# Splits of x queued behind the last gated block, a norm's offset subtracted in step with its sums, and the new tokens' matmuls placed in a row with cache visits

## The chip, the cores and the metric

The kernel runs on one core of one Trainium2 chip. The metric is the device time of one execution in microseconds (us). Before the change three runs took 1761.49, 1762.09 and 1762.12 us, median 1762.09. The profiled execution took 1763.11 us; its trace spans 1761.3 us from the first to the last instruction.

## What is computed

One layer of a decoder for 256 prompt tokens and 8 samples of 4 new tokens (288 tokens), in float32:

```
z = x @ w_in;  h, Bg, Cg, q, k, v, g_a, g_b = split(z)
ya = Bg * causal_conv3(Cg * h)
yb = dilated sliding-window attention(q, k, v, caches)        # 3 groups of 4 heads, dim 128
x1 = LN1(ALPHA*x + (sigmoid(g_a) * (ya @ w_a) + sigmoid(g_b) * (yb @ w_b)) @ w_out)
a, b = split(x1 @ w_up)
y  = LN2(ALPHA*x1 + (silu(causal_conv3(a)) * b) @ w_down)
```

The outputs are y for both groups, the last rows that enter each convolution, and the key and value windows: of the prompt, and of the samples with the new rows appended. Each sample attends to its cached keys (128 positions a group are used) and to the four new ones.

## The kernel before

**Tiling.** Activations lie by feature: 16 tiles of 128 features by 288 tokens (`KD` = 16, `T` = 288). A *product* is one output tile of 128 features for all 288 tokens. Each float32 operand is held as two parts, a rounded one (`hi`) and the rest (`lo`), and three matmuls make up one k step: hi·hi (L208), hi·lo of x (L209), lo·hi (L210). A product over 16 k steps is 48 matmuls of 128 x 128 by 288 columns. The names `acc` in the profile are the PSUM tiles of products.

**Weights.** `prepare` loads one weight block (1 MB, tile `wst`, three buffers) on SyncE's queue, and `half_block` splits each half: ScalarE casts it to `whi` (L138), VectorE subtracts for `wlo` (L139), four buffers of halves each. `product` prepares the next block when it takes one, so that a block is split while the one before it is multiplied. `split` (L213) does the same for activations, both instructions on L214.

**Order.** The program is written as if in one sequence, and a scheduler that estimates times decides the order of the instructions on each engine. `behind(i, after)` forces instruction i behind another on the same engine without a wait. `in_a_row` does this for a list of TensorE matmuls.

**Sample attention** (`sample_steps`, L406 to 496) is a generator; `product` advances it from time to time, so that its pieces stand between products. A *visit* is a row of matmuls that use two tiles of the key or value cache (tile `cache`, two buffers, 1 MB each, loaded and stored again on SyncE's queue by `fetch_two`). Their stationary operand has 32 columns, so four heads use the four column strips of the array (shape 128*32). Scores of the cached keys come from L421 into a `long` tile (one buffer); the scores of the new keys, `pn`, from L438, also in `long`; then the maximum, the exponential and the sum (L443 to 448), transposes (L451, L453, L461), and the sums over the values: L474 for the cache, L485 for the new tokens.

**FFN.** The hidden width of 44 tiles is worked in three parts (`THIRDS` = 16, 16, 12). In each part `gated` blocks are made first (two up products each, convolution, SiLU, gate; then `split` into `gh`, `gl`, which carry the names `yah`, `yal` in the profile), and then 16 down products add to the residual `dd`. In part 0 the input is LN1's argument not yet normalised (`x_gb`, with two more columns), and LN1 is applied behind the product (`normed`, L732); GpSimd and ScalarE normalise `dd` on the side (L773 to 775, one tile to a gated block). At the first down products the 16 tiles of `dd` are split into `x` for parts 1 and 2 (L781).

**LN2** is accumulated beside part 2's down products. `first` (L622) takes an offset c from tile 0. For tiles 1 to 15, GpSimd subtracts c from the residual (L785) before VectorE adds the product (L786); then `add` (L631) squares the tile on ScalarE (L635, tile `cy`, two buffers) and adds to the two sums on GpSimd (L639, L640). Behind the last product TensorE sums over the features (L648, L649), and `finish_out` normalises and stores y.

Of the kernel before, what the change touches and what calls it, by code (L numbers as in the profile page):

```python
# [13 lines left out]
ALU = mybir.AluOpType  # L14
# [3 lines left out]
P = 128  # L18
# [3 lines left out]
NB, NT = 8, 4  # L22
NS = NB * NT
# [10 lines left out]
NG, NH = 3, 4  # L34
# [49 lines left out]
def layer_kernel(ctx: ExitStack, tc: tile.TileContext, ins, outs):  # L84
# [14 lines left out]
    def sb(pl, shape, tag, dt=F32, bufs=None):  # L99
        return pl.tile(shape, dt, tag=tag, name=nm(tag), bufs=bufs)  # L100
# [4 lines left out]
    def h2(ap):  # L105
        return ap.rearrange("p (h a) -> p h a", h=2)
# [4 lines left out]
    def att(cols=512):  # L111
        return sb(ps, [P, cols], "att", bufs=2)

    def f32(ap):
        return ap.bitcast(F32)
# [13 lines left out]
    def copy_rest(after):  # L129
        if rest[0] < N_REST:  # L130
            n = rest[0]
            rest[0] += 1
            behind(sp.dma_start(outs["o_rest"][n], ins["rest"][n]), after)

    def half_block(st, k0, n):
        hi = sb(wp, [P, HK, P], "whi", F32R, bufs=4)
        lo = sb(wp, [P, HK, P], "wlo", F32R, bufs=4)
        act.copy(hi[:, :n, :], st[:, k0 : k0 + n, :])  # L138
        dve.tensor_tensor(lo[:, :n, :], st[:, k0 : k0 + n, :], f32(hi[:, :n, :]), ALU.subtract)  # L139
        return hi, lo, n  # L140

    def weight_list():
# [70 lines left out]
    def split(hi, lo, src):  # L213
        return act.copy(hi, src), dve.tensor_tensor(lo, src, f32(hi), ALU.subtract)  # L214
# [191 lines left out]
    def sample_steps():  # L406
        fetch_two()
        yield
        row = []
        s = sw2[:, :SW]  # L410
        sbias = cst[:, C_SB : C_SB + SW]
        for g in range(NG):
            qm = by_batch(q_s[:, g])
            cols = P if g == 0 else NT * P
            p = sb(ps, [P, cols], "long", bufs=1)
            for b in range(NB):
                if g > 0 or b % 4 == 0:
                    c = cache_tiles.pop(0)
                o = (b % 4) * NH * P if g == 0 else 0
                for j in range(NH):  # L420
                    row.append(pe.matmul(  # L421
                        p[j * NS : (j + 1) * NS], qm[:, j, b, :], c[:, o + j * cols : o + (j + 1) * cols],
                        start=b == 0, stop=b == NB - 1,
                    ))
                if b == NB - 1 or (g > 0 and b % 2 == 1):
                    in_a_row(row)
                    row = []
                    fetch_two()
                    yield
            sg = s[:, g * P : (g + 1) * P]  # L430
            if g == 0:
                dve.tensor_tensor(sg, p, sbias[:, :P], ALU.add)
            else:
                pick_t(sg, p, sbias[:, g * P : (g + 1) * P])
        pn = sb(ps, [P, NG * NS], "long", bufs=1)
        for j in range(NH):
            for g in range(NG):
                pe.matmul(  # L438
                    pn[j * NS : (j + 1) * NS, g * NS : (g + 1) * NS], q_s[:, g, j, :], k_s[:, g, j, :],
                    start=True, stop=True,  # L440
                )
        dve.tensor_tensor(s[:, NG * P :], pn, sbias[:, NG * P :], ALU.add)
        st = sb(wk, [P, 4], "st", bufs=4)  # L443
        dve.reduce_max(st[:, 0:1], s, AX.X)
        dve.tensor_scalar_mul(st[:, 1:2], st[:, 0:1], -SCALE)
        act.activation(s, s, AF.Exp, bias=st[:, 1:2], scale=SCALE, accum_out=st[:, 2:3])
        dve.reciprocal(st[:, 3:4], st[:, 2:3])
        dve.tensor_scalar_mul(s, s, st[:, 3:4])
        pt = att()
        for g in range(NG):  # L450
            pe.transpose(pt[:, g * P : (g + 1) * P], s[:, g * P : (g + 1) * P], ident)  # L451
        pt2 = att()
        pe.transpose(pt2[: NG * NS, :P], s[:, NG * P :], ident)  # L453
        sT = sw2[:, : NG * P].rearrange("p (g r) -> p g r", g=NG)
        act.copy(sT, pt[:, : NG * P].rearrange("p (g r) -> p g r", g=NG))
        sTn = sw2[: NG * NS, NG * P : NG * P + P]
        act.copy(sTn, pt2[: NG * NS, :P])
        vn = sw2[: NG * NS, NG * P + P : NG * P + P + NH * P].rearrange("p (j d) -> p j d", j=NH)
        pv = att()
        for j in range(NH):  # L460
            pe.transpose(pv[: NG * NS, j * P : (j + 1) * P], v_s[:, j].rearrange("p g r -> p (g r)"), ident)  # L461
        act.copy(vn, pv[: NG * NS].rearrange("p (j d) -> p j d", j=NH))
        o_sb = sw2[:, NG * P + P + NH * P : NG * P + 2 * P + NH * P]
        for g in range(NG):
            sm = by_batch(sT[:, g].rearrange("p (j r) -> p j r", j=NH))
            cols = P if g == 0 else NT * P
            if g < 2:
                p = sb(ps, [P, cols], "long", bufs=1)
            for b in range(NB):
                if g > 0 or b % 4 == 0:  # L470
                    c = cache_tiles.pop(0)
                o = (b % 4) * NH * P if g == 0 else 0
                for j in range(NH):
                    row.append(pe.matmul(  # L474
                        p[j * NS : (j + 1) * NS], sm[:, j, b, :], c[:, o + j * cols : o + (j + 1) * cols],
                        start=b == 0 and g < 2, stop=b == NB - 1 and g == 2,
                    ))
                if b == NB - 1 or (g > 0 and b % 2 == 1):
                    in_a_row(row)
                    row = []  # L480
                    fetch_two()
                    yield
            if g == 0:
                for j in range(NH):
                    pe.matmul(  # L485
                        p[j * NS : (j + 1) * NS], sTn[:, j * NS : (j + 1) * NS], vn[:, j, :], start=False, stop=True
                    )
                act.copy(o_sb, p)
            elif g == 2:
                pick_t(o_sb, p, o_sb)  # L490
        po = att(P)
        pe.transpose(po, o_sb, ident)
        oT = sw[:, :P]
        act.copy(oT, po)
        split(ybh[:, :, SEQ:], ybl[:, :, SEQ:], oT.rearrange("p (j r) -> p j r", j=NH))
        yield
# [117 lines left out]
    class Norm:  # L614
# [16 lines left out]
        def add(self, i):  # L631
            d = dd[:, i]
            last = i == KD - 1
            q = self.s2 if i == 0 else sb(wk, [P, T], "cy", bufs=2)
            act.activation(q, d, AF.Square)  # L635
            if i == 0:
                pool.tensor_copy(self.s1, d)
            elif not last or not self.tail:
                pool.tensor_tensor(self.s1, self.s1, d, ALU.add)  # L639
                pool.tensor_tensor(self.s2, self.s2, q, ALU.add)  # L640
            if i == KD - 2:

                act.activation(lw[:, 3, 0:1], q[:, 0:1], AF.Abs_reciprocal_sqrt)
            if last:
                self.p1, self.p2 = att(T), att(T)
                if self.tail:
                    for p, s, e in ((self.p1, self.s1, d), (self.p2, self.s2, q)):
                        pe.matmul(p, f32(ones_d), s, start=True, stop=False)  # L648
                        pe.matmul(p, f32(ones_d), e, start=False, stop=True)  # L649
                else:  # L650
                    w = sb(wk, [P, 4, T], "cache", F32R, bufs=2)
                    split(w[:, 0:2], w[:, 2:4], lw[:, 0:2])
                    for k in range(4):
                        pe.matmul((self.p1, self.p2)[k % 2], ones_d, w[:, k], start=k < 2, stop=k >= 2)

        def at(self, c, i):
            return prm[:, c + i : c + i + 1]
# [84 lines left out]
    cf = sb(big, [P, KF, 2 + 2 * NB], "qk_s")  # L742
    f = 0
    n2 = Norm(R_LN + 2 * KD, R_LN + 3 * KD, True)
    for part, nf in enumerate(THIRDS):
        gh = sb(big, [P, KD, T], "yah", F32R)
        gl = sb(big, [P, KD, T], "yal", F32R)
        for k in range(nf):
# [16 lines left out]
                gated(gf, y, *normed(pb))  # L765
            else:
                gated(gf, y, pb)
            split(gh[:, k], gl[:, k], gf)
            f += 1
            if part == 0:  # L770

# [6 lines left out]
        for i in range(KD):  # L778
            o = product((h3(gh), h3(gl)))
            if part == 0:  # L780
                split(x[0][:, i], x[1][:, i], h2(dd[:, i]))  # L781
                dve.scalar_tensor_tensor(h2(dd[:, i]), h2(dd[:, i]), ALPHA, o, ALU.mult, ALU.add)
            else:
                if f == KF and i > 0:
                    pool.tensor_tensor(dd[:, i], dd[:, i], n2.c, ALU.subtract)  # L785
                dve.tensor_tensor(h2(dd[:, i]), h2(dd[:, i]), o, ALU.add)  # L786
            if f == KF:
                if i == 0:
                    n2.first()
                n2.add(i)  # L790
    yf = sb(big, [P, KD, T], "yah")
    y_out = outs["o_y"].rearrange("p (k t) -> p k t", k=KD)
    n2.finish_out(yf, y_out)
# [183 lines left out]
```

## Time and profile before

| | before |
|---|---|
| median of 3 runs | 1762.09 us (1761.49 to 1762.12) |
| profiled execution | 1763.11 us, span 1761.3 us, 33600 instructions |
| granted TensorE clock, mean | 0.997 |
| HBM traffic over the span | 389.89 MB read, 94.53 MB written |

The page gives for each engine its busy time and share. PE is TensorE, DVE VectorE, ACT ScalarE, POOL GpSimd, SP SyncE. A row of a timeline gives the start in us from the span's start, the duration, the engine and the line of the kernel, the operation, and the tiles as output<-inputs; in square brackets stands the idle time before it and what ended that. Rows that repeat are merged (xN), and the duration then runs to the end of the last. Matmuls overlap, so their starts are what to compare. A matmul in plain float32 stands twice in the trace: the 12 small matmuls of L438 as 24.

### The profile page before, as it was taken

Reading aid. Unit: us, or ns where it says so; the run is one execution under the profiler, and the core shown is the slowest. Engines: PE = TensorE matmul, PEld = TensorE weight load, DVE = VectorE, ACT = ScalarE, POOL = GpSimd, SP = SyncE. Lnnn points to the kernel's source line nnn. Section 1 sums busy time; section 2 is a strip of 40 time slices with the busy share of each in tenths; the row PEclk is TensorE's granted clock in tenths of the full one; section 3 lists DMA queues with packets and bytes.
Section 4 is the critical chain, followed back from the end, with each engine's and each line's share of the span. In section 5 each row is a group of like instructions: output and inputs, shape, how many; then the busy total and the mean of one; then the engine's idle time right before and its main releaser. Section 6 shows DMA issues by size and latency. Waiting matters only on the chain.

```text
span 1761.3 us, 33600 instructions
## 1 busy us (share of the span) xinstructions
PE 1743.9 (99%) x14269; PEld 1714.4 (97%) x14269; DVE 1008.2 (57%) x1322; ACT 798.4 (45%) x1174; POOL 254.8 (14%) x403
## 2 busy tenths in 40 slices
PE   9999999999999999999999999999999999999996
PEld 9999999999999999999999999999999999999996
DVE  5444455545555444455588888774555554555554
ACT  5444444333434333344445656553454443345444
POOL 0000000000000000001155233310011110011174
PEclk9999999999999999999999999999999999999998
DMA  8477787787787887466766566656565656666662
GB/s 325 173 288 264 271 299 297 265 324 297 271 333 285 304 312 269 150 241 252 269 259 220 210 241 226 229 219 236 219 236 219 236 217 238 217 238 217 223 212 105
DMA packets 60919, 436.25 MB, mean 248 GB/s; under 512 B 7265, under 2 KB 8929, under 8 KB 16865
## 3 DMA queue, kind: packets, MB, share of 16 engines
q1 hardware_dynamic: 59040, 429.40, 65.9%
q10 hardware_dynamic: 1728, 4.72, 0.7%
q8 instruction: 111, 1.82, 0.4%
q14 instruction: 40, 0.32, 0.0%
HBM read 389.89 MB, written 94.53 MB: 275 GB/s over the span
## 4 chain that ended last, share of the span: by engine, by line
PE 96%; POOL 1%; ACT 1%; DVE 1%; issue 0%; DMA 0%; ACTq 0%; DVEq 0%
PE acc L208 31%; PE acc L210 31%; PE acc L209 31%; PE acc L276 1%; PE long L421 1%; PE long L474 1%; POOL dd L785 1%; PE att L362 0%; PE att L326 0%; ACT whi L138 0%; POOL qk_s L549 0%; ACT xh L214 0%; ACT yah L708 0%; DVE dd L684 0%; DMA yah<-in_x 0%
## 5 line engine op out<-in xcount | busy, mean ns | idle before, releaser
L139 DVE TENSOR_TENSOR wlo<-wst,whi 128x1024 fp32r<-128x1024 f32 (+1 forms) x578 | 706.9, 1224 | 617.3 <-ACT whi L138 613.2
L138 ACT CAST whi<-wst 128x1024 fp32r<-128x1024 f32 (+1 forms) x578 | 590.0, 1022 | 871.2 <-PE acc L209 767.7
L208 PE MATMUL acc<-xh,whi 128*128 128x288 f32 (+1 forms) x3216 | 923.0, 287 | 0.0
L210 PE MATMUL acc<-xh,wlo 128*128 128x288 f32 (+1 forms) x3216 | 920.5, 286 | 0.0
L209 PE MATMUL acc<-xl,whi 128*128 128x288 f32 (+1 forms) x3216 | 920.4, 286 | 0.0
L208 PEld LDWEIGHTS acc<-xh,whi 128*128 128x128 f32 x3216 | 607.8, 189 | 7.9 <-ACT h L569 2.5
L210 PEld LDWEIGHTS acc<-xh,wlo 128*128 128x128 f32 x3216 | 607.8, 189 | 0.8 <-issue 0.8
L209 PEld LDWEIGHTS acc<-xl,whi 128*128 128x128 f32 x3216 | 607.9, 189 | 0.3 <-issue 0.2
L208 PE MATMUL acc<-yah,whi 128*128 128x288 f32 x1216 | 348.0, 286 | 0.3 <-ACT yah L214 0.3
L210 PE MATMUL acc<-yah,wlo 128*128 128x288 f32 x1216 | 347.7, 286 | 0.6 <-DVE wlo L139 0.6
L209 PE MATMUL acc<-yal,whi 128*128 128x288 f32 x1216 | 347.6, 286 | 0.0
L208 PEld LDWEIGHTS acc<-yah,whi 128*128 128x128 f32 x1216 | 229.7, 189 | 3.1 <-ACT h L591 2.5
L210 PEld LDWEIGHTS acc<-yah,wlo 128*128 128x128 f32 x1216 | 229.8, 189 | 0.8 <-DVE wlo L139 0.8
L209 PEld LDWEIGHTS acc<-yal,whi 128*128 128x128 f32 x1216 | 229.8, 189 | 0.0
L549 POOL COPY qk_s<-u 128x2 f32<-128x2 f32 x44 | 41.5, 943 | 565.7 <-ACT u L758 441.1
L535 DVE SCALAR_TENSOR_TENSOR cy<-u,prm,cy 128x304 f32<-128x304 f32 x120 | 71.1, 593 | 3.4 <-ACT cy L533 0.7
L606 POOL TENSOR_TENSOR ya<-ya,dd 128x288 f32<-128x288 f32 x16 | 13.6, 851 | 306.0 <-DVE ya L605 306.0
L560 DVE TENSOR_TENSOR ya<-cy,acc 128x144 f32<-128x144 f32 x132 | 25.6, 250 | 33.6 <-PE acc L210 33.6
L549 POOL COPY cm<-u 128x2 f32<-128x2 f32 x16 | 3.0, 185 | 254.3 <-DVE u L574 254.3
L214 ACT CAST yah<-ya 128x288 fp32r<-128x288 f32 x76 | 32.7, 430 | 13.8 <-POOL ya L606 8.3
L214 DVE TENSOR_TENSOR yal<-ya,yah 128x288 fp32r<-128x288 f32 x76 | 34.9, 460 | 1.3 <-ACT yah L214 1.2
L639 POOL TENSOR_TENSOR cache<-cache,dd 128x288 f32<-128x288 f32 x29 | 28.0, 964 | 49.0 <-DVE dd L724 33.5
(179 smaller groups left out, 852.8 us busy)
## 6 DMA issues: line engine op xcount, KB each, us to landing
wst<-in_w_in SPq DMA_DIRECT2D x113, 1024.0 KB, 6.0
wst<-in_w_up SPq DMA_DIRECT2D x88, 1024.0 KB, 4.8
wst<-in_w_down SPq DMA_DIRECT2D x32, 1024.0 KB, 4.8
cache<-in_ck SPq DMA_DIRECT2D x18, 1024.0 KB, 6.4
out_o_ck<-cache SPq DMA_DIRECT2D x18, 1024.0 KB, 9.1
cache<-in_cv SPq DMA_DIRECT2D x18, 1024.0 KB, 6.3
out_o_cv<-cache SPq DMA_DIRECT2D x18, 1024.0 KB, 9.8
wst<-in_w_a SPq DMA_DIRECT2D x16, 1024.0 KB, 4.8
```

The source lines that it names most:

```text
L138: act.copy(hi[:, :n, :], st[:, k0 : k0 + n, :])
L139: dve.tensor_tensor(lo[:, :n, :], st[:, k0 : k0 + n, :], f32(hi[:, :n, :]), ALU.subtract)
L208: pe.matmul(out, hi[:, c, :], xh_k, start=k == 0, stop=False)
L209: pe.matmul(out, hi[:, c, :], xl_k, start=False, stop=False)
L210: last_mm[0] = pe.matmul(out, lo[:, c, :], xh_k, start=False, stop=k == nk - 1)
L214: return act.copy(hi, src), dve.tensor_tensor(lo, src, f32(hi), ALU.subtract)
L276: i = pe.matmul(o[b], first_w(term == 2, b, k), xk, start=k == 0 and term == 0, stop=k == KD - 1 and term == 2)
L421: row.append(pe.matmul(p[j * NS : (j + 1) * NS], qm[:, j, b, :], c[:, o + j * cols : o + (j + 1) * cols], start=b == 0, stop=b == NB - 1,))
L535: dve.scalar_tensor_tensor(y, u[:, i : i + YW], prm[:, w0 + i : w0 + i + 1], y, ALU.mult, ALU.add)
L549: pool.tensor_copy(dst[:, 0:2], u[:, SEQ : SEQ + 2])
L560: dve.tensor_tensor(a, b, c, ALU.mult)
L639: pool.tensor_tensor(self.s1, self.s1, d, ALU.add)
```

## The change

Four edits; none adds or takes away arithmetic.

- `half_block` uses `split` and keeps its two instructions in `w_split`.
- The splits of x in part 0's down products (L781) go behind the split of the last gated block (`last_split`) and behind that of the latest weight block, on ScalarE and VectorE each.
- The subtraction of c (L785) for tile i > 2 goes behind the sum of tile i - 3; `add` returns its last GpSimd instruction for this.
- The new tokens' matmuls L438 and L485 are appended to the row of the last key visit and of the first value visit. `pn` moves to an `att` tile (two buffers), and its loops are turned round, so that the four heads follow each other.

```
-        act.copy(hi[:, :n, :], st[:, k0 : k0 + n, :])
-        dve.tensor_tensor(lo[:, :n, :], st[:, k0 : k0 + n, :], f32(hi[:, :n, :]), ALU.subtract)
+        w_split[:] = split(hi[:, :n, :], lo[:, :n, :], st[:, k0 : k0 + n, :])
...
+                if g == NG - 1 and b == NB - 1:
+                    pn = att(NG * NS)
+                    row += [
+                        pe.matmul(
+                            pn[j * NS : (j + 1) * NS, k * NS : (k + 1) * NS], q_s[:, k, j, :], k_s[:, k, j, :],
+                            start=True, stop=True,
+                        )
+                        for k in range(NG) for j in range(NH)
+                    ]
...
-        pn = sb(ps, [P, NG * NS], "long", bufs=1)
-        for j in range(NH):
-            for g in range(NG):
-                pe.matmul(
-                    pn[j * NS : (j + 1) * NS, g * NS : (g + 1) * NS], q_s[:, g, j, :], k_s[:, g, j, :],
-                    start=True, stop=True,
-                )
...
+                if g == 0 and b == NB - 1:
+                    row += [
+                        pe.matmul(
+                            p[j * NS : (j + 1) * NS], sTn[:, j * NS : (j + 1) * NS], vn[:, j, :], start=False, stop=True
+                        )
+                        for j in range(NH)
+                    ]
...
             if g == 0:
-                for j in range(NH):
-                    pe.matmul(
-                        p[j * NS : (j + 1) * NS], sTn[:, j * NS : (j + 1) * NS], vn[:, j, :], start=False, stop=True
-                    )
                 act.copy(o_sb, p)
...
-                pool.tensor_copy(self.s1, d)
+                i_sum = pool.tensor_copy(self.s1, d)
...
-                pool.tensor_tensor(self.s2, self.s2, q, ALU.add)
+                i_sum = pool.tensor_tensor(self.s2, self.s2, q, ALU.add)
...
-            split(gh[:, k], gl[:, k], gf)
+            last_split = split(gh[:, k], gl[:, k], gf)
...
-                split(x[0][:, i], x[1][:, i], h2(dd[:, i]))
+                for i_x, *before in zip(split(x[0][:, i], x[1][:, i], h2(dd[:, i])), last_split, w_split):
+                    for b in before:
+                        behind(i_x, b)
...
-                    pool.tensor_tensor(dd[:, i], dd[:, i], n2.c, ALU.subtract)
+                    i_c = pool.tensor_tensor(dd[:, i], dd[:, i], n2.c, ALU.subtract)
+                    if i > 2:
+                        behind(i_c, sums[i - 3])
...
-                n2.add(i)
+                sums.append(n2.add(i))
```

More of the change, by code (lines that the diff above doesn't have):

```diff
@@ L133, in copy_rest @@
             behind(sp.dma_start(outs["o_rest"][n], ins["rest"][n]), after)
+    w_split = []
     def half_block(st, k0, n):
@@ L635, in add @@
             act.activation(q, d, AF.Square)
+            i_sum = None
             if i == 0:
-                pool.tensor_copy(self.s1, d)
+                i_sum = pool.tensor_copy(self.s1, d)
             elif not last or not self.tail:
                 pool.tensor_tensor(self.s1, self.s1, d, ALU.add)
-                pool.tensor_tensor(self.s2, self.s2, q, ALU.add)
+                i_sum = pool.tensor_tensor(self.s2, self.s2, q, ALU.add)
             if i == KD - 2:
@@ L654, in add @@
                         pe.matmul((self.p1, self.p2)[k % 2], ones_d, w[:, k], start=k < 2, stop=k >= 2)
+            return i_sum
         def at(self, c, i):
@@ L744, in layer_kernel @@
     n2 = Norm(R_LN + 2 * KD, R_LN + 3 * KD, True)
+    sums = []
     for part, nf in enumerate(THIRDS):
```

## The prediction

> **What bounds the kernel now.** I read the page's engine shares first, then the chain of waits, then TensorE's timeline wherever one of its matmuls starts later than a step after the one before, then the other engines' timelines at those places.
>
> ```profile
> span 1761.3 us, 33600 instructions
> ...
> PE 1743.9 (99%) x14269; PEld 1714.4 (97%) x14269; DVE 1008.2 (57%) x1322; ACT 798.4 (45%) x1174; POOL 254.8 (14%) x403
> ...
> PE   9999999999999999999999999999999999999996
> ```
>
> TensorE has work for all but 17.4 us of the span, and of that the last of the page's 40 slices (44 us each, busy to six tenths) holds most; the change touches nothing behind the last product. So no other engine's time counts by itself. The change can only win where TensorE stands still or runs badly packed matmuls, and only lose where it makes TensorE wait. Its normal step and the first badly packed place stand in one stretch of TensorE's timeline (columns: start, duration, engine, line, operation, count):
>
> ```profile
> 443.24 0.29 PE L209 MATMUL acc<-xl,whi 128*128 128x288 f32 x1
> ...
> 443.73 0.29 PE L210 MATMUL acc<-xh,wlo 128*128 128x288 f32 x1
> 443.94 0.65 PE L438 MATMUL long<-qk_s 128*32 128x32 f32 x24
> 444.52 0.39 PE L208 MATMUL acc<-xh,whi 128*128 128x288 f32 x1
> 444.74 0.29 PE L209 MATMUL acc<-xl,whi 128*128 128x288 f32 x1
> ```
>
> From 443.24 to 443.73 lie four steps, so a step is 0.1225 us (the durations overlap; starts are what to read). A product of 48 matmuls takes 5.88 us, one of the last stage (36) takes 4.41 us. The places where a start comes late are the working list; three edits address four of them.
>
> **New tokens' scores (L438).** Between the L210 at 443.73 and the L209 at 444.74 lie 1.01 us in which two ordinary matmuls (0.245 us) were done: the excursion costs 0.77 us. It consists of a late entry (0.216 us from 443.73 to 443.94), the 24 small matmuls with the change back (0.58 us to 444.52), and a long first step behind them. In the changed program's instruction order they stand directly behind the last visit to the key cache, whose tiles have the same 128*32 shape, so entry and exit are paid by the visit, which has both already. What stays is the 24 matmuls. Their price comes out of two other groups of this shape:
>
> ```profile
> 456.37 1.95 PE L474 MATMUL long<-cache,sw 128*32 128x128 f32 x64
> 458.26 0.39 PE L209 MATMUL acc<-xl,whi 128*128 128x288 f32 x1
> ```
>
> ```profile
> 476.86 0.29 PE L210 MATMUL acc<-xh,wlo 128*128 128x288 f32 x1
> 477.07 0.43 PE L485 MATMUL long<-sw 96*32 96x128 f32 x8
> 477.43 0.39 PE L208 MATMUL acc<-xh,whi 128*128 128x288 f32 x1
> 477.66 0.29 PE L209 MATMUL acc<-xl,whi 128*128 128x288 f32 x1
> ```
>
> 64 matmuls take 1.89 us to the next ordinary one and 8 take 0.36 us: four at a time, 16 rounds against 2, so a round is 1.53/14 = 0.109 us and the change back 0.14 us. Without it L438's group is 0.58 - 0.14 = 0.44 us. Bounds: rounds of four at a quarter of the 128-column price, 6 x 0.027 = 0.16 us, and the whole 0.58 us. I take 0.44, the group's own row, though its new order puts the four column groups next to each other. Gain 0.77 - 0.44 = 0.33 us (0.19 to 0.61). The Trainium skill ("TensorE: Matmul & The Clock Gate", section "Wait — 56ns, not 53.3ns?") puts a floor of about 25 ns under start-to-start, however small the matmul; by that the 24 would cost 0.60 us and the gain would be 0.17 us. The row, 24 in 0.44 us or 18 ns each, disagrees.
>
> **New tokens' values (L485).** The same reckoning: 476.86 to 477.66 is 0.80 us less two steps, 0.555 us. Joined to the value cache's first visit (L474, x64) it keeps two rounds, 0.22 us; if the 96-row tiles cost the change once more, 0.36 us. Gain 0.34 us (0.20 to 0.34).
>
> Bringing both forward moves what hangs on them. The softmax follows the scores by a few us where they stood 30 us later, and the visit with L485 comes one product earlier, some 450 us into the span. Queued behind it on ScalarE and VectorE are the copy of its sums and the second masked copy, then weight casts, as the masked copy is now; a weight cast has more than a product's time before its product. On SyncE two loads of the value cache and a store pass ahead of one weight load:
>
> ```profile
> 457.51 1.20 SPq L395 DMA_DIRECT2D cache<-in_cv  x2
> 463.70 0.34 SPq L396 DMA_DIRECT2D out_o_cv<-cache  x1
> 464.14 0.38 SPq L167 DMA_DIRECT2D wst<-in_w_in  x1
> ```
>
> Now too a store waits 6 us there for its load, with the weight load behind it, and no TensorE row after it is late: three weight buffers cover that. The same pattern moves one product forward. Without this cover it would cost up to 6 us; I count nothing.
>
> **Splits of x (about 1150 to 1170 us).** TensorE's timeline, then ScalarE's, GpSimd's and VectorE's:
>
> ```profile
> 1166.81 0.29 PE L209 MATMUL acc<-yal,whi 128*128 128x288 f32 x1
> 1167.44 0.51 PE L208 MATMUL acc<-yah,whi 128*128 128x288 f32 x2 [0.34 <-ACT yah L214]
> 1167.79 0.29 PE L210 MATMUL acc<-yah,wlo 128*128 128x288 f32 x1
> ```
>
> ```profile
> 1149.71 2.43 ACT L214 CAST xh<-dd 128x288 fp32r<-128x288 f32 x7
> ...
> 1161.56 0.63 ACT L775 ACTIVATE dd<-dd,prm 128x288 f32<-128x288 f32 x1 [3.73 <-POOL dd L774]
> ...
> 1166.96 0.43 ACT L214 CAST yah<-ya 128x288 fp32r<-128x288 f32 x1
> ```
>
> ```profile
> 1155.23 4.42 POOL L549 COPY qk_s<-u 128x2 f32<-128x2 f32 x1 [9.71 <-ACT u L754]
> ```
>
> ```profile
> 1155.44 3.03 DVE L214 TENSOR_TENSOR xl<-dd,xh 128x288 fp32r<-128x288 f32 x8
> ```
>
> Between the last gated block's steps the engines work off splits that nobody needs before part 1. GpSimd's two-column copy lasts 4.42 us, 3.03 of them while VectorE works off eight splits without a gap; ScalarE then waits 3.73 us for GpSimd; the block's own cast comes at 1166.96 and TensorE starts its last k late: 1166.81 to 1167.79 is 0.98 us for three steps (0.37), a loss of 0.61 us. In the changed order the first split stands behind that block's split and the others one to a product. The cast of the gated block before shows the undisturbed time:
>
> ```profile
> 1143.74 0.15 ACT L735 COPY wgb<-acc 128x2 f32<-128x2 f32 x1
> ...
> 1147.17 0.43 ACT L214 CAST yah<-ya 128x288 fp32r<-128x288 f32 x1 [0.37 <-DVE ya L563]
> ```
>
> That is 3.4 us behind its product; the first down product reaches its last k after 45 steps, 5.5 us, and the changed order gives it 11 steps more. So the stall should go: gain 0.61 us (0 to 0.61). The work moved is 16 casts and 16 subtractions, one pair to a product of 5.88 us:
>
> ```profile
> L139 DVE TENSOR_TENSOR wlo<-wst,whi 128x1024 fp32r<-128x1024 f32 (+1 forms) x578 | 706.9, 1224 | 617.3 <-ACT whi L138 613.2
> L138 ACT CAST whi<-wst 128x1024 fp32r<-128x1024 f32 (+1 forms) x578 | 590.0, 1022 | 871.2 <-PE acc L209 767.7
> ...
> L214 ACT CAST yah<-ya 128x288 fp32r<-128x288 f32 x76 | 32.7, 430 | 13.8 <-POOL ya L606 8.3
> L214 DVE TENSOR_TENSOR yal<-ya,yah 128x288 fp32r<-128x288 f32 x76 | 34.9, 460 | 1.3 <-ACT yah L214 1.2
> ```
>
> VectorE then does 2 x 1.22 + 0.46 for the split and about as much for the residual, 3.4 us, and ScalarE 2 x 1.02 + 0.43 = 2.5 us. Both lie under 5.88. The last split falls early in product 15 and part 1 starts behind that product.
>
> **c off the residual (about 1681 to 1705 us).**
>
> ```profile
> 1703.74 0.29 PE L209 MATMUL acc<-yal,whi 128*128 128x288 f32 x1
> 1704.62 0.39 PE L210 MATMUL acc<-yah,wlo 128*128 128x288 f32 x1 [0.60 <-DVE wlo L139]
> 1704.85 0.29 PE L208 MATMUL acc<-yah,whi 128*128 128x288 f32 x1
> ```
>
> ```profile
> 1681.88 15.96 POOL L785 TENSOR_TENSOR dd<-dd,cache 128x288 f32<-128x288 f32 x14 [13.56 <-ACT cache L628]
> ```
>
> ```profile
> 1699.75 0.44 ACT L635 ACTIVATE cy<-dd 128x288 f32<-128x288 f32 x1 [4.25 <-POOL cache L640]
> ...
> 1701.60 1.55 ACT L138 CAST whi<-wst 128x1024 fp32r<-128x1024 f32 x2
> ```
>
> GpSimd takes 14 subtractions in one go, 1.14 us each, before its first sum. A square (L635) has two buffers, so ScalarE waits 4.25 us for a sum, the weight cast behind it starts at 1701.60, and TensorE loses 1.11 - 0.245 = 0.865 us. The change lets GpSimd do one subtraction and two sums to a block. A subtraction then waits for the sum three blocks back, so it is still some two blocks (8 us) ahead of its use. Gain 0.865 us (0 to 0.865), with no operation more or less.
>
> **Sum.** 0.33 + 0.34 + 0.61 + 0.865 = 2.1 us. The profiled execution took 1763.11 us (span 1761.3), so that one would have taken 1761.0; it lies 1.0 us above the median of the runs, 1762.09. From that median: 1760.0 us. By the skill's 25 ns floor it would be 1760.1. The lower bounds of the packing alone (0.39) leave 1761.7; all upper bounds (2.4) give 1759.7.
>
> **Rivals.** (1) *GpSimd becomes the bound of the last stage.* It has to finish three operations in each block's 4.41 us, so this decides from 1.47 us an operation. Under VectorE's load they took, between 1702 and 1714 us:
>
> ```profile
> L640 POOL TENSOR_TENSOR cache<-cache,cy 128x288 f32<-128x288 f32 x5 | 6.4, 1283 | 0.0
> L639 POOL TENSOR_TENSOR cache<-cache,dd 128x288 f32<-128x288 f32 x5 | 5.9, 1181 | 0.1
> ```
>
> With 1.14 for the subtraction that is 3.6 us: it fits with 0.8 us to spare. For the rival speaks the 4.42 us copy, which VectorE's run of subtractions held up. At 1.8 us an operation, 5.4 a block, the lag would be 1 us a block, some 13 us at the end, where the last sums stand before the end's matmuls: about 1772 us. The Trainium skill ("SBUF — State Buffer", section "SBUF: two separate sides") has this as an exclusive lock between GpSimd and VectorE instructions with two SBUF inputs; the copy agrees with it. (2) *The stalls move.* Weight casts stay late for another reason (the value loads on SyncE, the copies behind the earlier visit, the last split of x), and only the packing stays: 1762.09 - 0.67 = 1761.4 us, or about 1762 where a new wait of the same size comes up. (3) *The order on paper isn't what limits*: one of the two stalls stays, because a release named by the profile was not the last. Then 1760.6 to 1760.9.
>
> **How the numbers follow.** Forecast 0.72, rival (3) 0.10, rival (2) 0.11, rival (1) 0.05, a gain beyond my bounds 0.02. The range runs from 1758.8 (upper bounds, and the 0.6 us over which the runs of before spread, and a little more) to 1762.2 (rival 2). A difference of 0.2%, 3.5 us, is about what a measurement of this kernel can tell from no change; the whole sum is 0.12%. Faster by more needs idle time that I don't see (0.05); slower by more needs rival (1), or 4 us of new waits (0.06); within it 0.89.
>
> **What would show it.** Right: no TensorE start over 0.3 us late between 1150 and 1170 or 1680 and 1710 us; GpSimd's subtractions spread over the last stage; ScalarE's squares without a wait for sums; one excursion fewer at the scores and at the values. Wrong: a TensorE wait for a weight cast near 450 us or at the start of part 1, GpSimd busy without a gap until the end's matmuls.

## The result and the profile after

| | before | after |
|---|---|---|
| median of 22 runs each | 1761.66 us (1761.33 to 1762.49) | 1759.36 us (1758.97 to 1760.76) |
| profiled execution | 1763.11 us, span 1761.3 us | 1759.85 us, span 1758.1 us |

The ratio of the times is 0.9987, with a 95% interval from 0.9981 to 0.9993. The medians lie 2.30 us apart. The time was forecast at 1760.0 us, with a gain of 2.1 us.

The page of the kernel after, its head with span and engine shares and the first line of the chain of waits (shares of the span by engine):

```profile
span 1758.1 us, 33617 instructions
...
PE 1740.6 (99%) x14269; PEld 1712.0 (97%) x14269; DVE 1008.8 (57%) x1322; ACT 799.9 (46%) x1174; POOL 248.3 (14%) x403
...
PE 99%; DMA 0%; DVE 0%; ACT 0%; SPq 0%; ACTq 0%; issue 0%; DVEq 0%
```

TensorE executes the same 14269 matmuls, and it makes up 99% of the chain. The span is 3.2 us shorter. Of this 0.86 us lies in the first 160 matmuls and is not owed to the change (see the experiments); the other 2.4 us went in two ways: packing (matmuls that start later behind each other than they need to) and stalls (waits of TensorE for another engine).

**Packing.** The kernel after, TensorE's timeline (start, duration, engine, line) around the last key visit, which now holds the new tokens' scores (L431, before L438):

```profile
412.51 1.04 PE L423 MATMUL long<-cache,sw 128*32 128x512 f32 x8
413.37 0.37 PE L431 MATMUL att<-qk_s 128*32 128x32 f32 x24
413.67 0.39 PE L210 MATMUL acc<-xh,whi 128*128 128x288 f32 x1
413.90 0.29 PE L211 MATMUL acc<-xl,whi 128*128 128x288 f32 x1
```

The excursion of its own, with the late entry of 0.216 us, is gone. And the 24 matmuls take 0.30 us up to the next ordinary one, where they took 0.58 us before. The same kernel around the first value visit, with the new tokens' values (L486, before L485):

```profile
448.83 0.29 PE L210 MATMUL acc<-xh,whi 128*128 128x288 f32 x1
449.05 1.95 PE L479 MATMUL long<-cache,sw 128*32 128x128 f32 x64
450.82 0.41 PE L486 MATMUL long<-sw 96*32 96x128 f32 x8
451.15 0.39 PE L211 MATMUL acc<-xl,whi 128*128 128x288 f32 x1
```

The visit takes 449.05 to 451.15, 2.10 us, where it took 1.89 us without the values: they cost 0.21 us now and 0.555 us before.

**Stalls.** No matmul row carries a wait between 1149 and 1172 us, and none between 1680 and 1710 us; the longest time from one start to the next is 0.124 us there, an ordinary step. What TensorE still waits for, by the view of waits (total us, times, longest), its first lines:

```profile
PE acc L228 <- DVE cy L225: 1.2, 1, 1.2
...
PE acc L278 <- ACT yal L216: 0.9, 2, 0.5
...
PE acc L278 <- ACT whi L216: 0.3, 1, 0.3
```

None of these lines touches the change: L228 and L278 belong to the kernel's first matmuls, and the wait of 1.2 us at L228 (before L226) stands in every trace here. The kernel after, ScalarE's timeline at the last gated block:

```profile
1154.47 0.63 ACT L787 ACTIVATE dd<-dd,prm 128x288 f32<-128x288 f32 x1
1155.80 1.05 ACT L216 CAST whi<-wst 128x1024 fp32r<-128x1024 f32 x1 [0.70 <-PE acc L211]
...
1157.22 0.43 ACT L216 CAST yah<-ya 128x288 fp32r<-128x288 f32 x1 [0.38 <-DVE ya L572]
1157.56 0.43 ACT L216 CAST xh<-dd 128x288 fp32r<-128x288 f32 x1
```

The wait of 3.73 us for GpSimd is gone, the block's cast stands at 1157.22 (before 1166.96), and the first split of x stands right behind it. GpSimd's two-column copy beside it shrank from 4.42 us to 0.83:

```profile
1151.42 0.83 POOL L558 COPY qk_s<-u 128x2 f32<-128x2 f32 x1 [7.67 <-ACT u L766]
```

In the last stage of the kernel after, GpSimd's timeline shows one block with its three operations, and the next block's first:

```profile
1711.51 1.11 POOL L649 TENSOR_TENSOR cache<-cache,dd 128x288 f32<-128x288 f32 x1 [1.75 <-DVE dd L802]
1712.58 0.79 POOL L650 TENSOR_TENSOR cache<-cache,cy 128x288 f32<-128x288 f32 x1
1713.33 0.80 POOL L799 TENSOR_TENSOR dd<-dd,cache 128x288 f32<-128x288 f32 x1
...
1715.92 1.11 POOL L649 TENSOR_TENSOR cache<-cache,dd 128x288 f32<-128x288 f32 x1 [1.79 <-DVE dd L802]
```

They take 2.6 us, and 1.79 us of a block are idle: GpSimd waits for the block, and no longer the block for GpSimd. ScalarE's squares (L644, before L635) now wait for VectorE's addition alone, where one of before's waited 4.25 us for a sum:

```profile
1698.65 0.44 ACT L644 ACTIVATE cy<-dd 128x288 f32<-128x288 f32 x1 [1.08 <-DVE dd L802]
```

### The profile page after: what moved, and what is told of

It reads as the page before. It is cut to its first block, busy times and chain, and to the rows that moved or that the text cites. A ratio compares the mean times of both kernels' runs of the same rounds, so it can differ in the third digit from the quotient of the medians.

```text
span 1758.1 us, 33617 instructions
## 1 busy us (share of the span) xinstructions
PE 1740.6 (99%) x14269; PEld 1712.0 (97%) x14269; DVE 1008.8 (57%) x1322; ACT 799.9 (46%) x1174; POOL 248.3 (14%) x403
## 4 chain that ended last, share of the span: by engine, by line
PE 99%; DMA 0%; DVE 0%; ACT 0%; SPq 0%; ACTq 0%; issue 0%; DVEq 0%
PE acc L210 31%; PE acc L212 31%; PE acc L211 31%; PE long L423 1%; PE long L479 1%; PE acc L278 1%; PE att L364 0%; DMA dd<-in_w_in 0%; PE att L328 0%; ACT yah L719 0%; DVE dd L695 0%; PE att L356 0%; PE att L348 0%; PE acc L328 0%; PE acc L356 0%; PE att L659 0%
## 5 line engine op out<-in xcount | busy, mean ns | idle before, releaser
L216 DVE TENSOR_TENSOR wlo<-wst,whi 128x1024 fp32r<-128x1024 f32 (+2 forms) x584 | 710.1, 1216 | 612.5 <-ACT whi L216 608.4
L216 ACT CAST whi<-wst 128x1024 fp32r<-128x1024 f32 (+2 forms) x584 | 593.3, 1016 | 874.1 <-PE acc L211 770.9
L558 POOL COPY qk_s<-u 128x2 f32<-128x2 f32 x44 | 37.8, 860 | 571.8 <-ACT u L770 449.2
```

The lines of the kernel that those rows point to most:

```text
L558: pool.tensor_copy(dst[:, 0:2], u[:, SEQ : SEQ + 2])
```

## The experiments

**How the parts are measured.** Every kernel here runs the same 14269 matmuls in nearly the same order. So the start of the Nth matmul in one trace can be set against the start of the Nth in before's trace. Such a *lead*, read at four places, tells each part by itself: at the 161st matmul (26.04 us in before) the start of the kernel is over, and behind the 4501st (545.18 us), 9701st (1184.57 us) and 14201st (1736.70 us) the places of the row edits, of the x splits and of c have been passed. What is gained at a place is the difference between two neighbouring columns. The device time bears the leads out: the time of the profiled execution less the start of its 161st matmul is 1737.07 us for before, and 2.40 us less for the changed kernel, 0.89, 0.57 and 0.85 us less for e1, e2 and e3, and 0.06 us more for before's twin e11.

| run | time, us (runs) | lead at 161 | at 4501 | at 9701 | at 14201 | rows / x / c |
|---|---|---|---|---|---|---|
| the change | 1759.36 (22) | 0.86 | 1.77 | 2.39 | 3.26 | 0.92 / 0.61 / 0.87 |
| e1_rows | 1761.23 (11) | 1.09 | 2.01 | 2.00 | 2.00 | 0.92 / 0 / 0 |
| e2_xsplit | 1761.45 (11) | -0.15 | -0.15 | 0.46 | 0.45 | 0 / 0.61 / 0 |
| e3_csub | 1761.23 (11) | 1.59 | 1.59 | 1.58 | 2.45 | 0 / 0 / 0.87 |
| e4_row_heads_outer | 1759.90 (1) | 1.06 | 1.73 | 2.33 | 3.21 | 0.67 / 0.61 / 0.87 |
| e5_apart_turned | 1762.23 (1) | 0.65 | 0.90 | 0.89 | 0.89 | 0.25 / 0 / 0 |
| e6_dd_behind | 1761.55 (1) | 0.93 | 0.94 | 1.55 | 1.55 | 0 / 0.61 / 0 |
| e7_x_at_once | 1759.93 (1) | 0.77 | 1.69 | 2.30 | 3.17 | 0.92 / 0.61 / 0.87 |
| e8_c_lag_one | 1759.89 (1) | 0.81 | 1.73 | 2.34 | 3.22 | 0.92 / 0.61 / 0.87 |
| e11_control | 1761.92 (11) | 1.06 | 1.06 | 1.04 | 1.02 | 0 / 0 / 0 |

**One part of the change alone** (e1 to e3). e1 is the kernel before with the two row edits, e2 with `half_block`, `last_split` and the splits of x, e3 with the subtraction of c: each takes its lines of the diff above and nothing else.

> The kernel before with the new tokens' matmuls joined to the visits alone. Theory (the parts are independent and TensorE's lost time is all that counts): the two excursions between 410 and 480 us are gone and the steps of TensorE from the last key visit to 480 us come 0.9 us earlier than before, counted by starts; both later stalls (0.61 us near 1165, 0.865 us near 1704) are still there; time 0.9 us under before. As the prediction had it: 0.67 us. Rival (the earlier visit makes weight casts late): a new TensorE wait behind 450 us, gain under 0.5 us.

> The kernel before with the splits of x queued behind the last gated block alone. Theory: the stall near 1165 us (0.61 us) goes, the one near 1704 us stays, both excursions stay; time 0.6 us under before. Rival (the stall moves to the start of part 1 or into the down products): TensorE waits somewhere between 1165 and 1260 us and the gain is under 0.3 us.

> The kernel before with the subtraction of c in step with the sums alone. Theory: the stall near 1704 us (0.865 us) goes, the rest stays; time 0.9 us under before. Rival (GpSimd bounds the stage): GpSimd without a gap up to the end's matmuls and TensorE waits between 1690 and 1745 us; no gain or slower.

By the traces each edit gains at its own place and nowhere else, and what it gains, 0.92, 0.61 and 0.87 us, is what it gains in the whole change. Their sum is 2.40 us. The times alone could not have told this: beside a median of 1761.55 us of before (27 runs) the ratios have intervals of 0.9988 to 1.0006 (e1 and e3) and 0.9990 to 1.0008 (e2), all three with 1, no change, inside, and the medians differ from before's by 0.32, 0.10 and 0.32 us, less than was expected. Only the profiled executions have a trace; that the other runs of e1 to e3 lost the rest at a later start is likely, but not shown.

Each of the three keeps the others' waits, as TensorE's view of waits shows. Of e1, which has both stalls:

```profile
PE acc L210 <- DVE wlo L139: 0.6, 1, 0.6
...
PE acc L208 <- ACT yah L214: 0.4, 1, 0.4
```

Of e2, only the wait for a weight part that belongs to c (L215 is the line of `split` there):

```profile
PE acc L211 <- DVE wlo L215: 0.6, 1, 0.6
```

**The same program again** (e11). The kernel before, unchanged, as a run of its own.

> The program of before once more, as a kernel of its own and timed like the three single edits. In the traces those take 0.9, 0.6 and 0.86 us off behind the first 160 matmuls, but in the times only 0.3, 0.1 and 0.3 us, and the first 160 matmuls end between 24.4 and 26.2 us from one execution to the next. Theory (a time is the sum of a start that differs by up to 1.8 us from execution to execution and a rest that repeats within 0.1 us; the single edits met later starts): this program's time differs from its twin's by 0.2 to 0.6 us too, and its trace behind the first 160 matmuls agrees with that of before within 0.1 us. Rival (the gains of the single edits in the traces aren't real, or start times belong to the program): the two times agree within 0.1 us.

It took 1761.92 us (11 runs) beside 1761.61 (15 runs), a ratio of 1.0002 with a 95% interval of 0.9993 to 1.0011. Two medians of one program differ by 0.31 us, as much as e1's or e3's from before's. From the 161st matmul on its trace agrees with before's within 0.04 us, matmul by matmul, over 1700 us.

**Which half of the row edit** (e4, e5). e4 is the changed kernel with the loops in before's order, e5 the kernel before with its loops turned and the matmuls left where they stood:

```
-                        for k in range(NG) for j in range(NH)
+                        for j in range(NH) for k in range(NG)
```

```
-        for j in range(NH):
-            for g in range(NG):
+        for g in range(NG):
+            for j in range(NH):
```

> The changed kernel, with the score matmuls of the new tokens still in the visit's row but in the loop order of before (heads outside, groups inside: three on one column strip in a row). It tells where the term that came out larger than forecast (0.58 us for 0.33 us) is from. Theory A (the turned loops are what makes the 24 matmuls cheap, 0.18 us for 0.44 us): the 24 take 0.4 to 0.45 us here, and the gain of this term falls to about 0.33 us. Theory B (standing in the row makes them cheap): they take 0.2 us as in the changed kernel.

> The kernel before, with only the loops of the score matmuls of the new tokens turned round (groups outside, heads inside); they stand apart from the visits as before. Theory A (the order makes the 24 cheap): the excursion near 444 us costs 0.77 - 0.25 = 0.5 us. Theory B (the row makes them cheap): 0.77 us as before.

TensorE's timeline of e4, then of e5:

```profile
413.17 0.62 PE L431 MATMUL att<-qk_s 128*32 128x32 f32 x24
413.72 0.39 PE L210 MATMUL acc<-xh,whi 128*128 128x288 f32 x1
```

```profile
443.29 0.40 PE L438 MATMUL long<-qk_s 128*32 128x32 f32 x24
443.62 0.39 PE L208 MATMUL acc<-xh,whi 128*128 128x288 f32 x1
```

In before's order the 24 matmuls take 0.55 us to the next ordinary one, joined to a visit; in the new order they take 0.33 us, standing apart. So the two effects are separate: the turned loops save 0.25 us (0.92 - 0.67, and e5 alone), joining the scores to the visit saves another 0.33, and the values 0.345.

**What made the last gated block late** (e6). The kernel before, with one order added: the normalising of `dd` for the last block goes behind that block's split on ScalarE, so ScalarE no longer waits for GpSimd ahead of it. No order is added on GpSimd and VectorE.

```
-            split(gh[:, k], gl[:, k], gf)
+            last_split = split(gh[:, k], gl[:, k], gf)
...
-                act.activation(dd[:, k], dd[:, k], AF.Identity, bias=n1.at(n1.b, k), scale=n1.at(n1.g, k))
+                i_dd = act.activation(dd[:, k], dd[:, k], AF.Identity, bias=n1.at(n1.b, k), scale=n1.at(n1.g, k))
+                if k == nf - 1:
+                    behind(i_dd, last_split[0])
```

> The kernel before, where ScalarE's last normalising of dd (L775, last tile), which waited 3.73 us for GpSimd, is queued behind the last gated block's own cast. Theory G (GpSimd's copy, held up by VectorE's run of subtractions, is what made the block late): without the wait the cast of the block comes some 3 us earlier and the 0.6 us stall near 1165 us goes. Theory V (the splits on VectorE and ScalarE themselves, in front of the block's steps, make it late): the stall stays at 0.3 to 0.6 us, though ScalarE doesn't wait for GpSimd.

GpSimd's timeline of e6 has the long copy unchanged:

```profile
1154.29 4.42 POOL L549 COPY qk_s<-u 128x2 f32<-128x2 f32 x1 [9.71 <-ACT u L754]
```

ScalarE's has this behind it:

```profile
1162.58 0.46 ACT L761 ACTIVATE cy<-cy 128x304 f32<-128x304 f32 x1 [4.76 <-DVE cy L535]
1162.94 1.03 ACT L138 CAST whi<-wst 128x1024 fp32r<-128x1024 f32 x1
1163.88 0.43 ACT L214 CAST yah<-ya 128x288 fp32r<-128x288 f32 x1
```

The cast stands at 1163.88, 3.1 us earlier than before's 1166.96, of which 0.94 is the earlier start of this trace: 2.1 us, less than expected, and enough to end the stall (0.61 us gained). So ScalarE's wait for GpSimd carried the stall to TensorE, not the copy as such. Two rows of before, VectorE's and ScalarE's, show how it got there:

```profile
1163.15 1.23 DVE L139 TENSOR_TENSOR wlo<-wst,whi 128x1024 fp32r<-128x1024 f32 x1 [2.28 <-ACT whi L138]
...
1165.66 0.46 ACT L761 ACTIVATE cy<-cy 128x304 f32<-128x304 f32 x1 [2.20 <-DVE cy L535]
```

ScalarE's next weight cast stood behind the wait, VectorE waited 2.28 us for that cast ahead of the block's own steps, and ScalarE waited for those before it could cast the block. Without the first wait ScalarE waits 4.76 us for VectorE instead: under it lay a second one, and the changed order has neither. The second one was the larger. Set against matmuls of the same number, the changed kernel has the cast 8.0 us earlier than before; e6 recovers 2.1 us of this, and the splits of x that VectorE works off ahead of the block take 1.55 + 1.19 + 3.03 = 5.8 us in before and in e6. e6's lateness does no harm because its first matmul that needs the block is the 100th of the down products (before the 102nd), at 1165.74 us; in the changed kernel the scheduler makes it the 57th, at 1159.64 us, with the cast done at 1157.66. That moving VectorE's splits alone would have ended the stall follows from these figures; no run tries it.

**Whether the splits have to be spread** (e7). The changed kernel without the order behind the weights' split:

```
-                for i_x, *before in zip(split(x[0][:, i], x[1][:, i], h2(dd[:, i])), last_split, w_split):
+                for i_x, *before in zip(split(x[0][:, i], x[1][:, i], h2(dd[:, i])), last_split):
```

> The changed kernel, with the splits of x only behind the last gated block's split and not behind the weights' split as well: most come in one go in the first down products. Theory (what counts is the gated block alone; weight splits have more than a product's slack): no stall near 1165 us, time as the changed kernel. Rival (a run of splits, 7 us on VectorE, makes weight splits late): a TensorE wait for a weight between 1160 and 1180 us, of up to some us.

VectorE's timeline of e7:

```profile
1158.70 4.14 DVE L216 TENSOR_TENSOR xl<-dd,xh 128x288 fp32r<-128x288 f32 x11
1162.76 0.45 DVE L796 SCALAR_TENSOR_TENSOR dd<-dd,acc 128x288 f32<-128x288 f32 x1
1163.12 1.92 DVE L216 TENSOR_TENSOR xl<-dd,xh 128x288 fp32r<-128x288 f32 x5
1164.96 2.35 DVE L216 TENSOR_TENSOR wlo<-wst,whi 128x1024 fp32r<-128x1024 f32 x2
```

All 16 subtractions run within 6.3 us, with one addition between them and the weights behind, and TensorE waits for nothing there: the gain stays 0.61 us. The order behind `last_split` is what counts; spreading over products gave nothing more here.

**The distance of c** (e8). The changed kernel with the subtraction directly behind the sums of the tile before:

```
-                    if i > 2:
-                        behind(i_c, sums[i - 3])
+                    behind(i_c, sums[i - 1])
```

> The changed kernel, with the subtraction of c behind the sum of the tile just before instead of three before. The subtraction for a tile then begins some 3 us behind the end of the block before it and is wanted 4.41 us behind that. Theory (GpSimd has 0.8 us to spare in a block): VectorE waits little or not at all for the subtraction, TensorE not at all, time as the changed kernel within 0.3 us. Rival (the distance of three is needed): VectorE's addition comes late in each block, and with it weight splits; TensorE waits, slower by 1 us or more.

The gain is the same 0.87 us. A distance of three is not needed.

**How much GpSimd can take in the last stage** (e12, e9, e10). The changed kernel with one, two or three more additions of the same shape to a block, kept in line behind its sums. They write rows that nobody reads. The edit for two, behind `sums.append(n2.add(i))`:

```
+                if 0 < i < KD - 1:
+                    i_e = pool.tensor_tensor(lw[:, 5], dd[:, i], n2.c, ALU.add)
+                    behind(i_e, sums[i])
+                    sums[i] = i_e
+                    i_e = pool.tensor_tensor(lw[:, 6], dd[:, i], n2.c, ALU.add)
+                    behind(i_e, sums[i])
+                    sums[i] = i_e
```

> The changed kernel with two more GpSimd additions (into rows that nothing reads) to each block of the last stage, so five operations of 128x288 to a block in place of three. It tests rival (1) of the prediction, where GpSimd bounds the stage from 4.41 us a block. Theory (an operation takes 0.8 us when VectorE rests and 1.2 us under its load): five take 4.0 to 4.6 us, GpSimd is busy without a gap, the lag at the end is under 3 us, TensorE waits under 1 us before its last matmuls. Rival (GpSimd and VectorE take turns strictly): weight splits on VectorE come late and TensorE waits in most blocks, slower by 5 us or more.

> The same with three more additions, six operations to a block. Theory: 4.8 us or more against 4.41, so GpSimd bounds the stage: 14 blocks x 0.4 to 1 us = 6 to 14 us of lag, of which some 2 us are slack, seen as waits of ScalarE's squares and of TensorE; 4 to 12 us slower than the changed kernel. Against it: no slowing at all would mean that GpSimd's time was never near the bound.

> The changed kernel with one more GpSimd addition to each block of the last stage: four operations where five took 5.28 us a block and three, with idle time between, 2.7 us. Theory (an operation costs 0.8 us plus what VectorE's run of 1.9 us in each block holds it up, about once or twice a block): four take 3.5 to 4.4 us, less than a block, and nothing is slower by over 0.3 us. Rival (1.06 us each and up, as with five, and the hold-ups grow): 4.5 us or more, a lag of 1 us and more at the end and TensorE waiting before its last matmuls.

GpSimd's timeline of e12, four operations to a block:

```profile
1710.10 1.78 POOL L649 TENSOR_TENSOR cache<-cache,dd 128x288 f32<-128x288 f32 x1
1711.84 1.24 POOL L650 TENSOR_TENSOR cache<-cache,cy 128x288 f32<-128x288 f32 x1
1713.04 0.80 POOL L808 TENSOR_TENSOR cache<-dd,cache 128x288 f32<-128x288 f32 x1
1713.80 0.80 POOL L799 TENSOR_TENSOR dd<-dd,cache 128x288 f32<-128x288 f32 x1
1714.56 1.78 POOL L649 TENSOR_TENSOR cache<-cache,dd 128x288 f32<-128x288 f32 x1
```

Of e9, five:

```profile
1709.96 1.85 POOL L799 TENSOR_TENSOR dd<-dd,cache 128x288 f32<-128x288 f32 x1
1711.77 0.80 POOL L649 TENSOR_TENSOR cache<-cache,dd 128x288 f32<-128x288 f32 x1
...
1715.25 1.85 POOL L799 TENSOR_TENSOR dd<-dd,cache 128x288 f32<-128x288 f32 x1
```

Four take 4.46 us to a block, without idle time and hardly more than the block's 4.41; the time was 1759.90 us, as in the single runs e4, e7 and e8 (1759.89 to 1759.93), and the leads give the changed kernel's 0.92, 0.61 and 0.87 us. Five take 5.29 us where at most 4.6 was expected, the sums fall behind from block to block, and e9 took 1770.88 us, 11.5 us over the changed kernel. TensorE was expected to wait under 1 us, and the rival's waits in most blocks didn't come either: the view of waits of e9 has most of the loss in one line, at the end's matmuls:

```profile
PE att L658 <- POOL cache L649: 7.9, 1, 7.9
```

With six, e10 took 1779.56 us, 20.2 us over the changed kernel, past what was expected. Its waits show a second place, late weight parts, 11 times:

```profile
PE att L658 <- POOL cache L649: 7.4, 1, 7.4
PE acc L212 <- DVE wlo L216: 5.3, 11, 0.8
```

So the rival's mechanism, GpSimd as the bound of the stage, exists at nearly the price that it was given (5.4 us a block and about 1772 us), and it begins to cost time between the fourth and the fifth operation to a block.

## Why the prediction was right

**The size as a whole.** Forecast 2.1 us; the medians say 2.30, and the leads behind the start 2.40. The one term that was mis-sized, 0.245 us at the scores, is the whole difference: 2.145 + 0.245 = 2.39. The forecast time, 1760.0 us, lies 0.64 us over the measured 1759.36; of this 0.43 is the base, since the median of before was 1762.09 us in three runs and 1761.66 in 22, and the rest is the gain. The forecast saw that before's profiled execution took 1.0 us more than the median and took the gain off the median. That was sound, as the excess lay in the start: the 161st matmul starts 0.65 to 1.6 us later there than in all but one of the other traces.

**Scores, the term that was mis-sized.** Forecast 0.33 us (0.19 to 0.61), measured 0.575 (0.92 less the values' 0.345). The step that failed is "I take 0.44, the group's own row, though its new order puts the four column groups next to each other". The entry, the way back and the long first step went as forecast (joining alone: 0.33). What the new order does to the 24 matmuls was written down and given nothing: it took 0.25 us by e4 and e5. The 24 then cost about 0.2 us (0.77 - 0.575), next to the lower of the two bounds, 0.16, that the rounds of four had given. The rule of the Trainium skill ("TensorE: Matmul & The Clock Gate", section "Wait — 56ns, not 53.3ns?"), a floor of some 25 ns from start to start, would have made it 0.17 us and is further off here: from the first to the last start the 24 take 0.175 us, 7.6 ns each. In before's order, with neighbours on one strip of columns (e4), they take 0.425 us, 18 ns each, nearer to that floor and still under it.

**Values.** Forecast 0.34 us, measured 0.345. Two rounds at the price taken from the value visit, 0.22 us, was the right count (they cost 0.21), and the 96-row tiles cost no change of shape.

**What hangs on the earlier softmax.** Counted as nothing, and e1 shows nothing: 2.01, 2.00 and 2.00 us of lead from the 4501st matmul on.

**Splits of x.** Forecast 0.61, measured 0.61. The chain in the prediction (splits, GpSimd's copy, ScalarE's wait, the block's cast) is one that carried the stall, as e6 tells it. It gives no time to the splits that VectorE works off ahead of the block's own steps, 5.8 us, which made the cast later still; the change moves them too, so the gain came out right. Its 45 and 11 steps are what the trace of the changed kernel has: the 57th of the down products' matmuls is the first that needs the block. That the splits go one to a product, which the working counted on for VectorE's load, is not what makes it safe: at once they did no harm (e7).

**c off the residual.** Forecast 0.865, measured 0.87. The squares no longer wait for sums, and TensorE's wait for the weight part behind them is gone.

**The rivals.** GpSimd as the bound: the prediction gave three operations 3.6 us of the block's 4.41, 0.8 to spare; they take 2.6 us and leave about 1.8. Its durations came from a stretch in which GpSimd worked without a gap; with idle time around them the same operations took 1.11, 0.79 and 0.80 us. At five operations the same limit is 0.88 us each, and five didn't fit: they take 5.29 us, with one of 1.24 and one of 1.85 us in each block. (The rival's 13 us on top of 1760.0 make 1773 us, not the 1772 that was written.) The stalls moved nowhere, and neither stayed, so the other two rivals fail.

**No change that a measurement can tell.** The difference of 0.13% lies inside the 0.2% that was called a tie, and the interval of 22 runs on each side still excludes no change. The prediction names no runs for its bound of 0.2%; with 22 on each side a smaller change shows.

## What to carry to other kernels

For edits worth less than the runs differ, set the starts of same-numbered matmuls of two traces against each other, behind the start: here it told each part to a few hundredths of a microsecond where medians of 11 runs told nothing. Price small matmuls by the order in which they use the column strips, not only by their shape, before moving them. Where an engine's queue holds work that nobody needs yet ahead of work that the next product needs, one order behind the urgent instruction is enough; look then for the next engine that is held by the same work.

## What the runs showed of the hardware

**Small matmuls on column strips.** In single records of the changed kernel the 24 matmuls start 6 to 9 ns apart within a round of four strips, and a round starts 29 to 32 ns behind the one before; from the first start to the last it is 0.175 us. In e4, with six records on one strip after each other, it is 0.425 us. In each of four traces (before, after, e4, e5) the next ordinary matmul starts 0.126 us behind the last small one, and its own step is 0.226 to 0.227 us where an ordinary one is 0.1225.

**The start differs from run to run.** The 161st matmul starts between 24.44 and 26.19 us over the fourteen traces, a scatter of 1.7 us beside a whole gain of 2.4 us. TensorE's timeline of before has this at 9 us:

```profile
8.77 0.69 PE L276 MATMUL acc<-xl,yal 128*128 128x288 f32 x2
9.25 0.45 PE L276 MATMUL acc<-xl,whi 128*128 128x288 f32 x1
```

And that of after, at the same place:

```profile
8.08 0.29 PE L278 MATMUL acc<-xl,whi 128*128 128x288 f32 x1
8.20 0.41 PE L278 MATMUL acc<-xh,cache 128*128 128x288 f32 x2
8.45 0.29 PE L278 MATMUL acc<-xh,wlo 128*128 128x288 f32 x1
```

Three matmuls take 0.37 us in after, a full-rate step each; in before two take 0.48, half the rate, and they do so until 10.7 us. By the clock records in the fourteen traces the full clock comes between 4.2 us (e12) and 10.8 us (e2). It comes by 7.4 us in all but two, before and e2, and these two have the latest 161st matmul, 26.04 and 26.19 us; the others lie between 24.44 and 25.39 us without following the clock (e12, the earliest step up, has 25.20), so something else differs at the start as well, and what it is stays open. The Trainium skill ("TensorE: Matmul & The Clock Gate", section "What's actually happening") describes a window of 3.4 us that runs freely, so that the moment of the step up varies from run to run, by half a microsecond either way. The traces agree in that it varies, but by 6.6 us from the earliest to the latest. They agree in the window too: the full clock lasts 1740.80 us in before and after, 1744.21 in e1 and 1737.38 in e2, lengths that lie 3.41 us apart.

**GpSimd beside VectorE.** One GpSimd operation on 128 x 288 takes 0.79 us, or 1.24, or 1.78 to 1.85, in one and the same block of e9 and e12, and the two-column copy 0.83 us or 4.42. The Trainium skill ("SBUF — State Buffer", section "SBUF: two separate sides") has an exclusive lock between GpSimd's instructions that read SBUF and VectorE's with two SBUF inputs, and these durations agree with it. For planning, the longer figures were the ones that came back as soon as GpSimd had no idle time.
